# Hybrid diffusion backbone on one core: a written order for the opening, one-column norm sums, and unread products in two waits

## The chip, the core and the metric

The kernel runs on one core of a Trainium2 chip. A core has five engines that work side by side: TensorE (PE in the rows: matrix products, with PEld its loads of the stationary operand), VectorE (DVE), ScalarE (ACT), GpSimd (POOL) and SyncE (SP, which issues the DMAs). The metric is device time in microseconds (us) from one launch to its end, the median over runs. Lower is better.

## What is computed

Two layers of a diffusion backbone run over 256 latent tokens behind 256 context tokens, 1024 channels each, in float32. Cut to what matters here:

```python
def rms_norm(x, g):
    y = x * lax.rsqrt(jnp.mean(x * x, axis=-1, keepdims=True) + EPS)
    return y * g
def adaln(x, g, shift, scale):
    return rms_norm(x, g) * (1 + scale) + shift
...
    mod_x = jax.nn.silu(c) @ w_mod[l] + b_mod[l]        # nine vectors of 1024 per layer, for latent
    mod_c = jax.nn.silu(c_ctx) @ w_mod[l] + b_mod[l]    # and for context tokens
...
    x += 0.5 * gate1 * SwiGLU_1(adaln_1(x))             # norm 0 of the layer
    h  = adaln_2(x)                                     # norm 1
    x += gate2 * W_o(sum_b sigmoid(G_b h) * P_b(mixer_b(h)))
    x += 0.5 * gate3 * SwiGLU_2(adaln_3(x))             # norm 2
```

The last layer needs only the latent tokens behind its mixer. There are six norms in all, (layer, 0 to 2); each divides every token by the root of its mean square over the 1024 channels.

## The kernel before

Channels lie on the 128 partitions and tokens along the rows: the stream x is eight tiles (chunks c = 0 to 7) of 128 channels by 512 tokens, columns 0 to 255 context (segment s = 0) and 256 to 511 latent (segment 1). Every large product is made of three products of halves of float32 (`mm3`, lines 191 to 193), so each weight tile is first split by ScalarE (`wh`, line 150) and VectorE (`wl`, line 151). Nearly all the work is such products; weights are fetched in one written sequence (`plan`).

**Order.** The code emits instructions in one sequence. Small jobs (norm chains, attention) are put between products by a virtual clock: `later(ns, fn)` runs a job once the products emitted since then add up to ns (a 256-column term counts 320), `yield ns` does the same inside a job. After that the framework's scheduler may still move instructions by its own estimate of when they can start, and each engine runs its list in order.

**A norm.** While the last product of a block finishes chunk c of segment s, `residual` (line 399) adds it to x on VectorE, `norm_square` (line 302 on) squares it on ScalarE and adds it up on GpSimd (line 307) into `acc`; for chunks 6 and 7 the square goes to TensorE instead. `norm_sum` multiplies with a 128x32 block of ones (line 318), so that the sums over channels stand in a row, twice per segment: once with acc and chunk 6, once with chunk 7. `norm_chain` then scales (326), turns the row into a column with a transpose (329), copies it (331), raises it to the power -1/2 on GpSimd (333), and spreads it over 128 rows by a product with the identity (337). `norm_apply` makes h and its low half for eight chunks (351 to 353). The last two chunks are finished segment by segment (`finish_stream`): context 6, context 7, latent 6, latent 7; then the next block starts on the context half. Only norm (1, 2) has one segment and nothing to run beside its chain.

**The opening.** Norm (0, 0) needs the first four of 18 sets of modulation vectors, which TensorE makes from 8 MB of weights (`mod_set`: 64 small products a set, line 265; a copy, 268; a transpose, 270). `first_tiles` runs the first two tiles of the first feed-forward block chunk by chunk as each set comes: 96 products of 512 columns in all. The order in which the small and the large products stand on TensorE is the scheduler's.

Of the kernel before, what the change touches and what calls it, by code (L numbers as in the profile page):

```python
# [16 lines left out]
D = 1024  # L17
# [18 lines left out]
class Net:  # L36
# [151 lines left out]

    def mm3(self, ps, wh, wl, xh, xl, first, last):
        mm = self.nc.tensor.matmul  # L190
# [8 lines left out]
    def consts(self):  # L199
# [9 lines left out]
        self.sc = self.cp.tile([128, 8, 32], F32, name="sc")  # L209
        self.rows = self.cp.tile([128, 2, 2, 512], F32, name="rows")  # L210
# [48 lines left out]
    def mod_set(self, l, s):  # L259
        nc = self.nc  # L260
        ps = self.ps("D", (128, 128))
        for k in range(KC):
            w = self.first[s, k][:].rearrange("p (g n) -> p g n", g=4)
            for g in range(4):
                nc.tensor.matmul(ps[32 * g:32 * g + 32, :], self.sc[:, k, :], w[:, g, :], start=(k == 0),  # L265
                                 stop=(k == KC - 1), tile_position=(0, 32 * g))
        sb = self.half()[:, 0:128]
        nc.scalar.activation(sb, ps, AF.Copy)
        pt = self.ps("E", (128, 4, 32))
        nc.tensor.transpose(pt[:].rearrange("p g n -> p (g n)"), sb, self.ident)  # L270
# [8 lines left out]
    def norm(self, l, i, rng):  # L279
        segs = self.segs(rng)  # L280
        n = dict(l=l, i=i, segs=segs, ps={}, R={}, acc={})
        n["H"] = [tuple(self.hp.tile([128, NT], F32R, name=self.nm("h"), tag="h") for _ in range(2)) for _ in range(KC)]
        return n

    def norm_stat(self, n, c, s):
        nc = self.nc
        if c == 0:
            n["ps"][s] = self.ps("DE"[s], (64, 128))
        sq = self.half()
        nc.scalar.activation(sq, self.x[c][:, 256 * s:256 * s + 256], AF.Square)  # L290
        for t in range(2):
            nc.tensor.matmul(n["ps"][s][32 * t:32 * t + 32, :], self.ones, sq[:, 128 * t:128 * t + 128],
                             start=(c == 0), stop=(c == KC - 1), tile_position=(0, 32 * t))

    def norm_square(self, n, c, s):
# [15 lines left out]
    def norm_sum(self, n, s, c, sq):  # L311
        nc = self.nc
        if c == 6:
            n["ps"][s] = self.ps("DE"[s], (64, 128))
        for t in range(2):
            w = slice(128 * t, 128 * t + 128)
            for p, v in enumerate((n["acc"][s], sq) if c == 6 else (sq,)):
                nc.tensor.matmul(n["ps"][s][32 * t:32 * t + 32, :], self.ones, v[:, w], start=(c == 6 and p == 0),
                                 stop=(c == 7), tile_position=(0, 32 * t))
        if c == 7:  # L320
            self.job(self.norm_chain(n, s), (n["l"], n["i"], s))

    def norm_chain(self, n, s, R=None):
        nc = self.nc
        ms = self.small((64, 128), "ms", 2)
        nc.vector.tensor_scalar(ms, n["ps"][s], 1.0 / D, EPS, op0=ALU.mult, op1=ALU.add)
        yield 500
        pt = self.ps("C" if R is None else "A", (128, 2, 32))
        nc.tensor.transpose(pt[:].rearrange("p g n -> p (g n)"), ms, self.ident[:64, :64])
        v = self.small((128, 2), "v4")  # L330
        nc.vector.tensor_copy(v, pt[:, :, 0])
        r = self.small((128, 2), "r4")
        nc.gpsimd.tensor_tensor(r, v, self.mhalf.to_broadcast([128, 2]), op=ALU.pow)
        yield 2500 if s else 1900
        n["R"][s] = self.ps("DE"[s], (128, 256)) if R is None else R
        for t in range(2):
            nc.tensor.matmul(n["R"][s][:, 128 * t:128 * t + 128], r[:, t:t + 1].to_broadcast([128, 128]), self.ident,
                             start=True, stop=True)
        if R is None:
            for c in range(KC):  # L340
                self.norm_apply(n, c, s)
# [13 lines left out]
    def first_norm(self):  # L355
# [5 lines left out]
        for s in range(2):  # L361
            for _ in self.norm_chain(n, s, R[:, 256 * s:256 * s + 256]):
                pass

        def step(j):
            self.mod_set(0, j)
# [6 lines left out]
    def first_tiles(self, W, P, H):  # L373

        def terms(m, j):
            for k in (2 * j, 2 * j + 1):
# [659 lines left out]
```

## Time and profile before

| | |
|---|---|
| median of three runs | 2041.42 us (2040.87 to 2042.23) |
| the profiled execution, its own time | 2040.34 us |
| span in that profile | 2038.6 us |
| TensorE busy | 2010.8 us, 99% of the span |
| VectorE busy | 1331.3 us, 65% |
| ScalarE busy | 800.3 us, 39% |
| GpSimd busy | 87.3 us, 4% |
| DMA | 295.50 MB, mean 145 GB/s |
| mean granted TensorE clock | 0.997 of full speed |

Times inside the program are counted from the start of the span. A matmul's row shows its start and its modelled length; since matmuls overlap, what one costs is read from the distance between starts. Full speed of the granted clock is 2.4 GHz, and 0.50 is its other level, 1.2 GHz.

### The profile page before, as it was taken

To read this page: it belongs to the slowest core of one execution; us is meant where nothing else is said; L and a number is where in the kernel's file an instruction comes from. 1 tells how busy PE (TensorE), PEld (TensorE's weight loads), DVE (VectorE), ACT (ScalarE), POOL (GpSimd) and SP (SyncE) were. 2 spreads that over 40 slices of the span, in tenths; PEclk is the share of its full clock that TensorE was granted. 3 is DMA by queue.
4 is the path that set the end of the run, shared out by engine and by line. 5 is a ranking of instruction groups with operands and counts; after the bars stand their busy time and mean duration, and the time that the engine had idled before them with its cause. 6 is when DMAs were issued, how large, how long until landed. Compare 5 with 4: busy or idle time off the path is not lost.

```text
span 2038.6 us, 29838 instructions
## 1 busy us (share of the span) xinstructions
PE 2010.8 (99%) x11765; PEld 1732.7 (85%) x11765; DVE 1331.3 (65%) x2914; ACT 800.3 (39%) x1311; POOL 87.3 (4%) x90
## 2 busy tenths in 40 slices
PE   7999999999999999999999999999999999999999
PEld 4888887897797788888888888888888999999999
DVE  4878986667555545685733358689844788775554
ACT  3332232356444434232222333222323676664443
POOL 0000000120010000100000010000002101010000
PEclk9999999999999999999999999999999999999999
DMA  9554653522222224244532233446434324463453
GB/s 350 167 212 172 223 207 125 180 68 60 70 91 76 78 94 154 83 166 152 186 106 90 72 139 145 173 168 237 179 125 131 86 91 136 152 231 141 169 191 121
DMA packets 61549, 295.50 MB, mean 145 GB/s; under 512 B 14689, under 2 KB 16353, under 8 KB 38241
## 3 DMA queue, kind: packets, MB, share of 16 engines
q1 hardware_dynamic: 61408, 293.60, 41.4%
q8 instruction: 92, 1.51, 0.3%
q14 instruction: 49, 0.39, 0.1%
HBM read 292.53 MB, written 1.05 MB: 144 GB/s over the span
## 4 chain that ended last, share of the span: by engine, by line
PE 93%; DVE 3%; issue 2%; DMA 1%; ACT 1%; POOL 0%; SPq 0%; POOLq 0%; ACTq 0%; DVEq 0%
PE A L191 19%; PE A L192 18%; PE A L193 18%; PE B L191 11%; PE B L192 11%; PE B L193 11%; DVE a L249 1%; PE B L668 1%; PE D L682 1%; PE C L648 1%; PE E L719 1%; DVE wl L151 1%; DMA w<-in_dn 0%; ACT wh L150 0%; PE D L265 0%
## 5 line engine op out<-in xcount | busy, mean ns | idle before, releaser
L150 ACT ACTIVATE wh<-w 128x1024 fp32r<-128x1024 f32 (+2 forms) x476 | 428.1, 905 | 863.7 <-PE A L192 333.5
L151 DVE TENSOR_TENSOR wl<-w,wh 128x1024 fp32r<-128x1024 f32 (+2 forms) x476 | 490.1, 1033 | 286.5 <-ACT wh L150 283.6
L191 PE MATMUL A<-h,wh 128*128 128x512 f32 (+1 forms) x1440 | 506.9, 352 | 5.8 <-ACT wh L150 3.3
L193 PE MATMUL A<-h,wl 128*128 128x512 f32 (+1 forms) x1440 | 496.2, 345 | 1.2 <-DVE wl L151 1.1
L192 PE MATMUL A<-h,wh 128*128 128x512 f32 (+1 forms) x1440 | 496.3, 345 | 0.7 <-DVE h L353 0.7
L249 DVE CUSTOM_DVE_ANT_0 a<-w,rows 128x512 f32<-128x512 f32 x512 | 350.4, 695 | 41.1 <-DMA w<-in_mod 32.3
L191 PEld LDWEIGHTS A<-h,wh 128*128 128x128 f32 x1440 | 273.2, 190 | 48.3 <-issue 11.5
L193 PEld LDWEIGHTS A<-h,wl 128*128 128x128 f32 x1440 | 273.4, 190 | 35.1 <-DVE wl L151 2.5
L192 PEld LDWEIGHTS A<-h,wh 128*128 128x128 f32 x1440 | 273.5, 190 | 31.8 <-DVE h L353 1.4
L191 PE MATMUL B<-h,wh 128*128 128x512 f32 (+1 forms) x736 | 262.2, 356 | 0.0
L193 PE MATMUL B<-h,wl 128*128 128x512 f32 (+1 forms) x736 | 261.7, 356 | 0.0
L192 PE MATMUL B<-h,wh 128*128 128x512 f32 (+1 forms) x736 | 261.7, 356 | 0.0
L191 PEld LDWEIGHTS B<-h,wh 128*128 128x128 f32 x736 | 139.8, 190 | 19.9 <-ACT wh L150 0.4
L192 PEld LDWEIGHTS B<-h,wh 128*128 128x128 f32 x736 | 139.7, 190 | 19.6 <-issue 0.4
L193 PEld LDWEIGHTS B<-h,wl 128*128 128x128 f32 x736 | 139.6, 190 | 19.6
L432 DVE TENSOR_TENSOR t<-t,B 128x512 f32<-128x512 f32 (+1 forms) x88 | 54.2, 619 | 107.4 <-PE B L193 106.4
L307 POOL TENSOR_TENSOR nb<-nb,l 128x256 f32<-128x256 f32 x45 | 47.2, 1066 | 1320.0 <-ACT l L305 1320.0
L191 PE MATMUL A<-b,wh 128*128 128x512 f32 (+1 forms) x246 | 85.4, 347 | 1.0 <-ACT wh L150 1.0
L193 PE MATMUL A<-b,wl 128*128 128x512 f32 (+1 forms) x246 | 85.1, 346 | 1.1 <-DVE wl L151 1.1
L192 PE MATMUL A<-b,wh 128*128 128x512 f32 (+1 forms) x246 | 84.9, 345 | 0.0
L191 PE MATMUL B<-b,wh 128*128 128x512 f32 (+1 forms) x204 | 73.1, 358 | 0.4 <-ACT wh L150 0.4
L193 PE MATMUL B<-b,wl 128*128 128x512 f32 (+1 forms) x204 | 73.1, 358 | 0.3 <-DVE wl L151 0.3
(266 smaller groups left out, 2927.4 us busy)
## 6 DMA issues: line engine op xcount, KB each, us to landing
w<-in_gu SPq DMA_DIRECT2D x88, 1024.0 KB, 4.9
w<-in_mod SPq DMA_DIRECT2D x64, 1024.0 KB, 4.8
w<-in_dn SPq DMA_DIRECT2D x64, 704.0 KB, 4.1
w<-in_gb SPq DMA_DIRECT2D x64, 640.0 KB, 3.8
w<-in_fm SPq DMA_DIRECT2D x10, 1024.0 KB, 4.8
w<-in_tm SPq DMA_DIRECT2D x10, 1024.0 KB, 5.0
w<-in_wo SPq DMA_DIRECT2D x8, 1024.0 KB, 4.8
b<-in_first SPq DMA_DIRECT2D x20, 256.0 KB, 6.2
```

Of the source, the lines that this page charges most:

```text
L150: nc.scalar.activation(hi[i][:, :e], t[:, o:o + e], AF.Copy)
L151: nc.vector.tensor_tensor(lo[i][:, :e], t[:, o:o + e], hi[i][:, :e].bitcast(F32), op=ALU.subtract)
L191: mm(ps, wh, xh, start=first, stop=False)
L192: mm(ps, wh, xl, start=False, stop=False)
L193: mm(ps, wl, xh, start=False, stop=last)
L249: nc.vector.tensor_tensor_reduce(out=junk, in0=w[:, g, k], in1=self.rows[:, v, k], scale=1.0, scalar=0.0, op0=ALU.mult, op1=ALU.add, accum ...
L307: nc.gpsimd.tensor_tensor(n["acc"][s], n["acc"][s], sq, op=ALU.add)
L432: nc.vector.tensor_tensor(s[:, lo:hi], s[:, lo:hi], ps[1][:, lo:hi], op=ALU.mult)
L648: nc.tensor.transpose(pt[:, j], p[:, 128 * j:128 * j + 128], self.ident)
L668: nc.tensor.matmul(S[hh][:, 256 * j:256 * j + 256], queries(sg, j)[rows, pr, qw], keys(j, pr)[rows], start=True, stop=True)
L682: nc.tensor.matmul(y[64 * hh:64 * hh + 64, 128 * qb:128 * qb + 128], value(j, pr, hh), T[u, hh][:, j], start=(j == 0), stop=(j == n - 1), ...
L719: nc.tensor.matmul(pz[:, 256 * s:256 * s + 256], bd[:, 4 * j + k], U[c][:, src], start=True, stop=True)
```

## The change

It has four parts, and no weight, DMA or large product is added or left out.

1. **Opening.** `mod_set` is split into `mod_sums` (small products and copy) and `mod_set` (transpose and what follows), and `first_tiles` writes the order out by hand. While `pinned` is set, all its matmuls keep the written order. The spread of the first norm (`first_factors`) uses transposes.
2. **Norm sums.** In all later norms the 128 tokens become the stationary operand and one column of ones is multiplied, so that the sums come out as a column at once. The transpose and the copy of it go, and the spread (two products in two passes each) becomes two transposes of a broadcast column.
3. **GpSimd adds.** Norms behind feed-forward blocks (`pool`: norm 1 of both layers and norm 0 of layer 1) add all chunks on GpSimd and have one sum per segment; norm 2 adds chunks 0 to 6 there and gives the sum acc and chunk 7. The virtual waits become 2300 (or 1100) and 2600 or 4500.
4. **Unread products.** `warm(n, tag)` multiplies the identity by itself n times into a tile that nobody reads: 14 times while the first weights are split, and three times 5 in the chain of the one-segment norm (`alone`).

```diff
+    def pin(self, ins):
+        return self.tc.keep_in_program_order(ins)
...
-    def mod_set(self, l, s):
+    def mod_sums(self, s):
         nc = self.nc
         ps = self.ps("D", (128, 128))
         for k in range(KC):
             w = self.first[s, k][:].rearrange("p (g n) -> p g n", g=4)
             for g in range(4):
-                nc.tensor.matmul(ps[32 * g:32 * g + 32, :], self.sc[:, k, :], w[:, g, :], start=(k == 0),
-                                 stop=(k == KC - 1), tile_position=(0, 32 * g))
+                self.pin(nc.tensor.matmul(ps[32 * g:32 * g + 32, :], self.sc[:, k, :], w[:, g, :], start=(k == 0),
+                                          stop=(k == KC - 1), tile_position=(0, 32 * g)))
         sb = self.half()[:, 0:128]
         nc.scalar.activation(sb, ps, AF.Copy)
+        return sb
...
+    def token_sums(self, n, s, v, first, last):
+        if first:
+            n["ps"][s] = self.ps("DE"[s], (128, 2))
+        for t in range(2):
+            for i, q in enumerate(v):
+                self.nc.tensor.matmul(n["ps"][s][:, t:t + 1], q[:, 128 * t:128 * t + 128], self.ones[:, 0:1],
+                                      start=first and i + t == 0, stop=last and i + t == len(v))
+    def warm(self, n, tag):
+        t = self.ps(tag, (128, 128))
+        for _ in range(n):
+            self.pin(self.nc.tensor.matmul(t, self.ident, self.ident, start=True, stop=True))
...
+    def factors(self, n, s, v, R):
+        r = self.small((128, 2), "r4")
+        nc.gpsimd.tensor_tensor(r, v, self.mhalf.to_broadcast([128, 2]), op=ALU.pow)
+        n["R"][s] = R
+        return [lambda t=t: nc.tensor.transpose(R[:, 128 * t:128 * t + 128], r[:, t:t + 1].to_broadcast([128, 128]),
+                                                self.ident) for t in range(2)]
...
-        if c < 6:
+        if c < 7 or n["pool"]:
             nc.gpsimd.tensor_tensor(n["acc"][s], n["acc"][s], sq, op=ALU.add)
+        if c == 7:
+            v = [n["acc"][s]] if n["pool"] else [n["acc"][s], sq]
+            self.later(2300 if n["pool"] else 1100, lambda: self.norm_sum(n, s, v))
+    def norm_sum(self, n, s, v):
+        if n["alone"]:
+            self.warm(5, "D")
+        self.token_sums(n, s, v, True, True)
+        self.job(self.norm_chain(n, s), (n["l"], n["i"], s))
+    def norm_chain(self, n, s):
+        v = self.small((128, 2), "v4")
+        nc.vector.tensor_scalar(v, n["ps"][s], 1.0 / D, EPS, op0=ALU.mult, op1=ALU.add)
+        spread = self.factors(n, s, v, self.ps("DE"[s], (128, 256)))
+        if n["alone"]:
+            self.warm(5, "D")
         else:
-            self.later(1100, lambda: self.norm_sum(n, s, c, sq))
+            yield 4500 if s else 2600
+        for f in spread:
+            f()
+        if n["alone"]:
+            self.warm(5, "D")
...
-        self.first_step(0)
-        for j in range(4):
-            terms(0, j)
-            if j < 3:
-                self.first_step(j + 1)
-            terms(1, j)
+        self.pinned = True
+        self.first_step(0, self.mod_sums(0))
+        self.warm(14, "E")
+        terms(0, 0, 1)
+        terms(1, 0, 1)
+        self.first_step(1, self.mod_sums(1))
+        sb = self.mod_sums(2)
+        terms(0, 2)
+        self.first_step(2, sb)
+        terms(0, 3)
+        terms(1, 2, 3)
+        sb = self.mod_sums(3)
+        terms(0, 4)
+        self.first_step(3, sb)
+        terms(0, 5)
+        terms(1, 4, 5)
+        terms(0, 6, 7)
+        terms(1, 6, 7)
+        self.pinned = False
```

What this does to the lists of the engines is shown at three places. In the rows below, a name is a tile with its number, left of the arrow what is written and right of it what is read; the shape is the output.

First, TensorE in the opening, where the second set of modulation vectors (D_411 here) meets the first tile pair, before:

```order
L193 MATMUL B_341<-h_187,wl_317 128x512
L265 MATMUL D_411<-b_137,sc 32x128 x4
L265 MATMUL D_411<-b_139,sc 32x128 x4
L191 MATMUL A_342<-h_185,wh_322 128x512
L265 MATMUL D_411<-b_141,sc 32x128 x4
L192 MATMUL A_342<-h_186,wh_322 128x512
L193 MATMUL A_342<-h_185,wl_324 128x512
L191 MATMUL B_343<-h_185,wh_323 128x512
L265 MATMUL D_411<-b_143,sc 32x128 x4
L192 MATMUL B_343<-h_186,wh_323 128x512
```

The same set after the change (D_438), behind the last of the 24 products of chunks 0 and 1; the transpose of its copy is line 282:

```order
L196 MATMUL B_343<-h_187,wl_325 128x512
L273 MATMUL D_438<-b_137,sc 32x128 x4
L273 MATMUL D_438<-b_139,sc 32x128 x4
L273 MATMUL D_438<-b_141,sc 32x128 x4
L273 MATMUL D_438<-b_143,sc 32x128 x4
L273 MATMUL D_438<-ya_145,sc 32x128 x4
L273 MATMUL D_438<-ya_147,sc 32x128 x4
L273 MATMUL D_438<-ya_149,sc 32x128 x4
L273 MATMUL D_438<-ya_151,sc 32x128 x4
L282 MATMUL E_473<-cst,l_471 128x128
L273 MATMUL D_493<-yp_153,sc 32x128 x4
```

The small products stood between the large ones in pieces of four and now stand together; the transpose stands directly behind them.

Second, TensorE at norm (1, 0), context segment, while latent chunk 6 runs; before, the sum of chunk 7 and, six products on, the transpose (the sum of acc and chunk 6 stood further up):

```order
L193 MATMUL A_9832<-b_9018,wl_9752 128x256
L318 MATMUL D_9882<-l_9909,ones 32x128 x2
L191 MATMUL A_9832<-b_9085,wh_9750 128x256
L192 MATMUL A_9832<-b_9086,wh_9750 128x256
L193 MATMUL A_9832<-b_9085,wl_9752 128x256
L191 MATMUL A_9832<-b_9152,wh_9750 128x256
L192 MATMUL A_9832<-b_9153,wh_9750 128x256
L193 MATMUL A_9832<-b_9152,wl_9752 128x256
L329 MATMUL C_9933<-cst,ms_9925 128x64
```

After, the one sum of that segment, 24 products behind chunk 7's last (12 before):

```order
L196 MATMUL A_9825<-m_9279,wh_9744 128x256
L196 MATMUL A_9825<-m_9280,wh_9744 128x256
L196 MATMUL A_9825<-m_9279,wl_9746 128x256
L303 MATMUL D_9925<-ones,nb_9530 128x1 x2
L196 MATMUL A_9825<-m_9346,wh_9744 128x256
```

One sum of acc alone (nb) stands where two sums and a transpose stood before.

Third, TensorE at the one-segment norm (1, 2), before, from the last product of chunk 7 to the first of the next block:

```order
L193 MATMUL B_16316<-a_16082,yp_16230 128x256
L318 MATMUL E_16356<-l_16374,ones 32x128 x2
L329 MATMUL C_16384<-cst,ms_16382 128x64
L337 MATMUL E_16390<-cst,r_16388 128x128 x2
L191 MATMUL A_16378<-h_12878,wh_16239 128x256
```

The same place after the change:

```order
L196 MATMUL B_16285<-a_16051,yp_16199 128x256
L310 MATMUL D_16345<-cst 128x128 x5
L303 MATMUL E_16351<-ones,nb_16091 128x1
L303 MATMUL E_16351<-ones,l_16339 128x1
L303 MATMUL E_16351<-ones,nb_16091 128x1
L303 MATMUL E_16351<-ones,l_16339 128x1
L310 MATMUL D_16361<-cst 128x128 x5
L339 MATMUL E_16358<-cst,r_16359 128x128 x2
L310 MATMUL D_16369<-cst 128x128 x5
L196 MATMUL A_16343<-h_12850,wh_16208 128x256
```

Unread products now stand in each of the three waits of that chain, and the transpose (329) is gone.

## Rows read from the trace of the kernel before

**Rows 1.** First part of the page: busy time, share, instructions.

```profile
PE 2010.8 (99%) x11765; PEld 1732.7 (85%) x11765; DVE 1331.3 (65%) x2914; ACT 800.3 (39%) x1311; POOL 87.3 (4%) x90
```

**Rows 2.** Windows: length, busy us of each engine, granted clock, DMA.

```profile
20.50:27.30 6.80, 5.80 (x20) 3.91 (x24) 6.01 (x8) 4.30 (x6) 0.00 (x0) 0.50 1.02 371
60.77:350.00 289.23, 289.23 (x1277) 239.56 (x1276) 235.96 (x572) 80.21 (x103) 0.00 (x0) 1.00 0.53 189
1843.20:1846.60 3.40, 3.04 (x14) 3.04 (x15) 3.40 (x10) 2.58 (x6) 0.00 (x0) 0.50 0.00 0
```

**Rows 3.** Timeline of TensorE, opening: start, length, instruction, idle before.

```profile
21.50 0.80 PE L191 MATMUL A<-h,wh 128*128 128x512 f32 x1 [3.34 <-ACT wh L150]
...
27.72 0.49 PE L191 MATMUL A<-h,wh 128*128 128x512 f32 x1
28.14 0.43 PE L265 MATMUL D<-b,sc 128*32 128x128 f32 x8
28.50 0.50 PE L192 MATMUL A<-h,wh 128*128 128x512 f32 x1
...
34.35 0.33 PE L270 MATMUL E<-cst,l 128*128 128x128 f32 x1 [0.46 <-ACT l L268]
...
48.78 1.51 PE L265 MATMUL D<-b,sc 128*32 128x128 f32 x46
...
60.77 0.40 PE L191 MATMUL A<-h,wh 128*128 128x512 f32 x1
```

**Rows 4.** Timeline of VectorE, opening: the last weight splits of the first pair.

```profile
24.15 2.36 DVE L151 TENSOR_TENSOR wl<-w,wh 128x1024 fp32r<-128x1024 f32 x2
```

**Rows 5.** Timeline of TensorE at two norms: products around each interruption.

```profile
426.32 0.28 PE L193 MATMUL A<-h,wl 128*128 128x256 f32 x1
...
426.78 0.28 PE L192 MATMUL A<-h,wh 128*128 128x256 f32 x1
...
1203.07 0.28 PE L193 MATMUL A<-b,wl 128*128 128x256 f32 x1
...
1203.85 0.28 PE L192 MATMUL A<-b,wh 128*128 128x256 f32 x1
...
1206.87 0.28 PE L193 MATMUL B<-b,yp 128*128 128x256 f32 x1
...
1207.55 0.28 PE L192 MATMUL B<-b,ya 128*128 128x256 f32 x1
...
1208.38 0.28 PE L193 MATMUL B<-b,yp 128*128 128x256 f32 x1
...
1209.38 0.28 PE L192 MATMUL B<-b,ya 128*128 128x256 f32 x1
...
1217.82 0.28 PE L192 MATMUL B<-h,wh 128*128 128x256 f32 x1
...
1218.46 0.28 PE L191 MATMUL A<-h,wh 128*128 128x256 f32 x1
...
1218.70 0.28 PE L193 MATMUL A<-h,wl 128*128 128x256 f32 x1
1219.33 0.71 PE L337 MATMUL E<-cst,r 128*128 128x128 f32 x4 [0.35 <-POOL r L333]
```

**Rows 6.** Timeline of TensorE, norm (0, 2), context segment.

```profile
834.07 0.30 PE L318 MATMUL D<-l,ones 128*32 128x128 f32 x1 [1.71 <-ACT l L305]
```

**Rows 7.** Timeline of TensorE at the one-segment norm (1, 2).

```profile
1838.20 0.28 PE L193 MATMUL B<-a,yp 128*128 128x256 f32 x1
1839.56 0.41 PE L318 MATMUL E<-l,ones 128*32 128x128 f32 x4 [1.08 <-ACT l L305]
...
1841.67 0.71 PE L337 MATMUL E<-cst,r 128*128 128x128 f32 x4 [1.04 <-POOL r L333]
1843.56 0.58 PE L191 MATMUL A<-h,wh 128*128 128x256 f32 x1 [1.18 <-ACT h L352]
```

**Rows 8.** Instructions of two lines: count, ns least/median/most, first and last start.

```profile
L307 POOL TENSOR_TENSOR nb<-nb,l x45: 729/1074/1472, 354.7 to 1833.5; 128x256 f32<-128x256 f32 x45
L249 DVE CUSTOM_DVE_ANT_0 a<-w,rows x512: 671/691/1232, 62.6 to 1488.0; 128x512 f32<-128x512 f32 x171
```

More of the change, by code (lines that the diff above doesn't have):

```diff
@@ L209, in consts @@
         self.sc = self.cp.tile([128, 8, 32], F32, name="sc")
+        self.sv = self.sc[:, :, 0:2]
         self.rows = self.cp.tile([128, 2, 2, 512], F32, name="rows")
@@ L264, in mod_set @@
             for g in range(4):
-                nc.tensor.matmul(ps[32 * g:32 * g + 32, :], self.sc[:, k, :], w[:, g, :], start=(k == 0),
-                                 stop=(k == KC - 1), tile_position=(0, 32 * g))
+                self.pin(nc.tensor.matmul(ps[32 * g:32 * g + 32, :], self.sc[:, k, :], w[:, g, :], start=(k == 0),
+                                          stop=(k == KC - 1), tile_position=(0, 32 * g)))
         sb = self.half()[:, 0:128]
         nc.scalar.activation(sb, ps, AF.Copy)
+        return sb
+    def mod_set(self, l, s, sb):
+        nc = self.nc
         pt = self.ps("E", (128, 4, 32))
-        nc.tensor.transpose(pt[:].rearrange("p g n -> p (g n)"), sb, self.ident)
+        self.pin(nc.tensor.transpose(pt[:].rearrange("p g n -> p (g n)"), sb, self.ident))
         bm = self.par[l][:, O_BM + 4 * s:O_BM + 4 * s + 4]
@@ L280, in norm @@
         segs = self.segs(rng)
-        n = dict(l=l, i=i, segs=segs, ps={}, R={}, acc={})
+        n = dict(l=l, i=i, segs=segs, ps={}, R={}, acc={}, pool=i != 2, alone=len(segs) == 1)
         n["H"] = [tuple(self.hp.tile([128, NT], F32R, name=self.nm("h"), tag="h") for _ in range(2)) for _ in range(KC)]
         return n
+    def token_sums(self, n, s, v, first, last):
[9 more added lines that the diff above has]
+            self.pin(self.nc.tensor.matmul(t, self.ident, self.ident, start=True, stop=True))
     def norm_stat(self, n, c, s):
@@ L293, in norm_stat, with first_factors @@
                              start=(c == 0), stop=(c == KC - 1), tile_position=(0, 32 * t))
+    def first_factors(self, n, s, R):
+        nc = self.nc
+        ms = self.small((64, 128), "ms", 2)
+        nc.vector.tensor_scalar(ms, n["ps"][s], 1.0 / D, EPS, op0=ALU.mult, op1=ALU.add)
+        pt = self.ps("A", (128, 2, 32))
+        nc.tensor.transpose(pt[:].rearrange("p g n -> p (g n)"), ms, self.ident[:64, :64])
+        v = self.small((128, 2), "v4")
+        nc.vector.tensor_copy(v, pt[:, :, 0])
+        for f in self.factors(n, s, v, R):
+            f()
+    def factors(self, n, s, v, R):
+        nc = self.nc
+        r = self.small((128, 2), "r4")
[3 more added lines that the diff above has]
+                                                self.ident) for t in range(2)]
     def norm_square(self, n, c, s):
@@ L305, in norm_square @@
         nc.scalar.activation(sq, x, AF.Square)
-        if c < 6:
+        if c < 7 or n["pool"]:
             nc.gpsimd.tensor_tensor(n["acc"][s], n["acc"][s], sq, op=ALU.add)
-        else:
-            self.later(1100, lambda: self.norm_sum(n, s, c, sq))
[L311 to L341, printed above, removed]
+        if c == 7:
+            v = [n["acc"][s]] if n["pool"] else [n["acc"][s], sq]
+            self.later(2300 if n["pool"] else 1100, lambda: self.norm_sum(n, s, v))
@@ new lines, in norm_sum @@
+    def norm_sum(self, n, s, v):
[4 more added lines that the diff above has]
+    def norm_chain(self, n, s):
+        nc = self.nc
+        v = self.small((128, 2), "v4")
+        nc.vector.tensor_scalar(v, n["ps"][s], 1.0 / D, EPS, op0=ALU.mult, op1=ALU.add)
+        spread = self.factors(n, s, v, self.ps("DE"[s], (128, 256)))
+        if n["alone"]:
+            self.warm(5, "D")
+        else:
+            yield 4500 if s else 2600
+        for f in spread:
+            f()
+        if n["alone"]:
+            self.warm(5, "D")
+        for c in range(KC):
+            self.norm_apply(n, c, s)
+        if n["alone"]:
+            yield 0
@@ L361, in first_norm, with step @@
         for s in range(2):
[L362 to L366, printed above, removed]
+            self.first_factors(n, s, R[:, 256 * s:256 * s + 256])
+        def step(j, sb):
+            self.mod_set(0, j, sb)
             for c in (2 * j, 2 * j + 1):
@@ L373, in first_tiles, with terms @@
     def first_tiles(self, W, P, H):
-        def terms(m, j):
-            for k in (2 * j, 2 * j + 1):
+        def terms(m, *ks):
+            for k in ks:
                 for g in range(2):
                     self.term(P[m][g], W[m], 1024 * g, H, *ALL, k)
-        self.first_step(0)
-        for j in range(4):
-            terms(0, j)
-            if j < 3:
-                self.first_step(j + 1)
-            terms(1, j)
+        self.pinned = True
[17 more added lines that the diff above has]
+        self.pinned = False
     def finish_stream(self, parts, last, add, nxt):
```

3 lines of the change are left out of this document (2 added, 1 removed).

## The prediction

> **What bounds it now.** I read the engine table first. TensorE is busy 99% of the span and VectorE 65% [rows 1], so only two things can move the time: what TensorE executes beside the large products, and the places where it runs slowly or waits. The windows show both. From 60.77 to 350.00 us TensorE has not one idle moment: 289.23 us busy over 1277 products of 512 columns, 0.2265 us each, at a granted clock of 1.00, while VectorE is busy 82% [rows 2]. Two short stretches differ: 20.50 to 27.30 us, with 5.80 us of work at clock 0.50, and 1843.20 to 1846.60 us, with 3.04 us, also at 0.50 [rows 2]. The first lies behind a wait of 3.34 us, the second behind three waits of 1.08, 1.04 and 1.18 us [rows 3, 7]. The timeline of TensorE then gives the cost of every interruption as the distance between the products around it. The change touches three such places, the opening, six norms and one of these six that stands alone. I cost each and add them up.
>
> **The opening.** From the first large product (21.50) to the first of the third tile (60.77) it lasts 39.27 us [rows 3]. In it stand 96 products of 512 columns, 96 × 0.2265 = 21.7 us, and the sums of three sets, 192 passes. A run of 46 takes 1.51 us, one pass alone about 0.27 by its shape, so 0.0276 us for each further one [rows 3], 5.3 us together. The other 12.2 us are loss, of three kinds. The clock: the 5.80 us of work at half speed would take 2.9, loss 2.9 us. Switching: from 27.72 to 28.50 stand one large product and 8 small ones, 0.78 us where 0.23 + 0.22 would do: 0.33 us for each interruption. There are 14 such groups up to 48.78, two of them shown [rows 3]; loss 4.6 us. The rest, 4.7 us, is waiting, for copies (0.46 at 34.35) and for h.
>
> After the change the small products of a set stand together: three interruptions, 1.0 us. The 28 unread passes (14 products of two) at the 0.11 us of an fp32 pass of 128 columns (0.45 / 4, below) take 3.1 us and so fit inside the 3.34 us wait. If they keep the clock up the 2.9 us come back. But the first products are then too early for their weights: the splits of the first pair end at 26.51, and the third and fourth of them run 1.18 us each from 24.15 [rows 4]. Laying 24 products at 0.2265 against these ends gives about 28.1 instead of 26.9 us for the last, 1.2 us lost. The three copies and transposes now stand ahead of products in a fixed order, so I keep the waits as they are, 4.4 us with that 1.2 in it. The loss falls from 12.2 to 5.4, and the third tile starts at 54.0: **gain 6.8 us**. Bounds: nothing, if the fixed order waits as often as the free one switched, and 12 if all loss goes. Since TensorE never idles from 60.77 to 350 [rows 2], an earlier start arrives later in full, as long as VectorE, with its 82%, keeps up.
>
> **The norm sums.** Two neighbouring products are 0.23 us of normal distance over two steps (2 × 0.2265 / 2). What exceeds it is the price, all from [rows 5]. The sum of acc and chunk 6 costs 1.00 − 0.23 = 0.77, the sum of chunk 7 0.78 − 0.23 = 0.55, the transpose of the row 0.64 − 0.23 = 0.41, the spread with its four passes 0.68 − 0.23 = 0.45, thus 0.11 for a pass. Ahead of the latent spread comes a wait, 0.63 − 0.11 = 0.52, of which its row puts 0.35 on GpSimd's power.
>
> A segment costs 2.18 us, the latent one 2.70. Four norms have two segments: 4 × 4.88 = 19.5, and norm (0, 2) waited 1.71 us more for the square of a chunk [rows 6]: 21.2 us before.
>
> After, a spread is two transposes of 128 columns; a pair of those costs 0.46 − 0.23 = 0.23 [rows 5]. No row shows a one-column product with 128 stationary rows. It lies between the 0.0276 us of a small pass [rows 3] and 0.22, if load and product lie one behind the other at 0.11 each. I take 0.11, the price of a 128-column pass, because loading 128 stationary columns is then the longer part. The three GpSimd norms have per segment two products of two passes, 0.45, and the spread 0.23: 6 × 0.68 = 4.1. The remaining norm has four products, 0.90 + 0.23, twice: 2.3. Together 6.4 us, a saving of 14.8.
>
> New waits come off. In the written order the sum at a GpSimd norm stands 24 products behind chunk 7's last, 24 × 0.113 = 2.7 us. In that time residual, square and a GpSimd add of 0.73 to 1.47 us, median 1.07 [rows 8], must pass. The add leaves the other two 1.2 us or more, which may just do, and I leave 0.1 us for each of six. In norm (0, 2) the first sum stands 12 products back and the second spread 8 behind its sum, 0.9 us against a scale, a power and their turns: 0.5 each. That makes 1.6 us. **Gain 13.2 us.** Bounds of the pass price on 48 passes: 4 us more (0.0276), 5.3 less (0.22).
>
> **The lone norm (1, 2).** From its last product to the next block 5.36 us pass (1838.20 to 1843.56), in three waits of 1.08, 1.04 and 1.18 [rows 7]. Five unread products are 10 passes, 1.1 us at full clock: they fit each wait. If the clock stays up, the 3.40 us window at 0.50 shrinks to half: 1.7 us. The chain loses the transpose and its copy (0.41 plus a turn), and 0.22 of spread, and gets two more sum passes: about 0.6 shorter. The early sum of acc and chunk 6 (0.77) goes. **Gain 3.1 us.** Bounds: 1.4, if the clock still falls, to 4.
>
> **Sum.** 6.8 + 13.2 + 3.1 = 23.1 us. The profiled execution took 2040.34, 1.74 above its span, and lies 1.08 below the median of the runs. So 2040.34 − 23.1 = 2017.2, and as a median 2018.3 us. VectorE loses 12 instructions, SyncE's list keeps its order, ScalarE's nearly; GpSimd goes from 4% of the span to some 5%, with 15 adds of 1.1 us more [rows 1, 8]. None of these is a price by itself.
>
> **Rivals.** The clock is not held (0.10): unread products or the order leave the granted clock at 0.50 in 21 to 27 us and at 1843. Against it: TensorE fell to 0.50 behind a wait of 3.34 us and behind waits of about 1.1 in a row [rows 2, 3, 7], and these are filled. For it: the fill is inferred at 0.11 a pass, and if shorter, a wait is left. Loss: 2.9 + 1.7, and the 58 unread passes at half clock take 0.11 more each, 6.4 us, of which half may stick out of the waits: 2023 to 2026.
>
> GpSimd and VectorE hinder each other (0.12). GpSimd's adds range from 0.73 to 1.47 us and VectorE's modulation rows, usually 0.69, reach 1.23 [rows 8]. If 15 more adds each cost VectorE 0.54 and all of it came onto TensorE, that is 8.1 us: 2026.4. Against it: in most norms VectorE has slack. The Trainium skill ("SBUF — State Buffer", section "SBUF: two separate sides") says that the port pair which VectorE and GpSimd share is an exclusive lock, taken against each other by a GpSimd operation and a VectorE operation with two SBUF inputs, and that the loser fully blocks. The spread of those two rows agrees with such a lock, but no row shows it, and the residuals that lead into the sums are of that kind.
>
> The opening's gain is swallowed (0.10): modulation products, paced by transfers or by VectorE at 82%, stall TensorE further on. Against it: no idle from 60.77 to 350 [rows 2]. Price 6.8: 2025.1.
>
> Slower than before (0.02). TensorE's list has its order, and when it comes to a sum the latent residual of chunk 7 still queues on VectorE behind the 13 or so operations (by the order) that normalise the context half; square and GpSimd add follow, and TensorE stands. It decides from a wait of about 4.5 us at each of six sums: (23.1 + 4) / 6. Against it: 51 products, 5.8 us, lie between the end of chunk 7 and the latent sum. With 5 us each: 2018.3 + 30 = 2048.
>
> The written order brings nothing in the opening and the lone norm (0.05): 2018.3 − 13.2 kept, the rest lost: 2028.
>
> **Chances and range.** My forecast has 0.61. About 0.2% or 4 us is what a measurement of this kernel can tell from no change. All cases but the slower one, and small mixtures of two misses, lie more than 4 us below 2041.42: faster 0.95, same 0.03, slower 0.02. The range of the forecast alone is 2014 to 2024 (pass price, −4 to +5.3). With the opening's upper bound at the low end and the rivals at 2023 to 2028 in it, and about one tenth left out at each end, it is 2013 to 2029.
>
> **What would show it.** Granted clock 1.00 through 17 to 28 us and at 1843; third tile at about 54; no transpose of the row, sum groups at 0.45 and 0.90; waits for GpSimd ahead of spreads gone, except about 0.5 at norm (0, 2); at norm (1, 2) about 4.7 us from last to first product; TensorE without idle from 54 to 345. I am wrong if sums or unread passes cost over 0.2 us each, if an idle stretch appears at the new sums, or if the third tile starts after 58.

## The result, and the profile after

The changed kernel takes **2020.64 us** (median of four runs, 2020.27 to 2021.12), against 2041.26 us for the kernel before in the same session: a ratio of 0.9898 with a 95% interval from 0.9886 to 0.9910, 20.6 us less. The forecast was 2018.3, with a range from 2013 to 2029. The span of the profiled execution falls from 2038.6 to 2019.2 us.

Both traces hold the same 10,518 large products on TensorE. Numbering them in order of time and subtracting the start of the k-th one after from that of the k-th one before gives the lead of the changed kernel, and the places at which it grows:

| place | lead grows by | forecast |
|---|---|---|
| opening (5.03 us at the third tile's first product, 5.47 from 58 us on) | 5.47 us | 6.8 us |
| norm (0, 1) | 2.69 | |
| norm (0, 2) | 3.79 | |
| norm (1, 0) | 2.30 | |
| norm (1, 1) | 2.73 | |
| these four norms together | 11.51 | 13.2 |
| attention of the second layer | −0.24 | 0 |
| norm (1, 2), one segment | 2.46 | 3.1 |
| all | 19.2 | 23.1 |

Between these places the lead stays constant to 0.05 us, but for swings between 355 and 375 us that cancel. The rows of the changed kernel follow. First the page's engine table and three windows (length, then busy us of PE, PEld, DVE, ACT, POOL, the granted clock, DMA share and GB/s), which answer to [rows 1, 2]:

```profile
PE 1997.5 (99%) x11732; PEld 1732.6 (86%) x11732; DVE 1329.5 (66%) x2905; ACT 799.8 (40%) x1311; POOL 102.5 (5%) x105
```

```profile
20.50:27.30 6.80, 6.09 (x32) 4.63 (x31) 6.10 (x8) 4.46 (x6) 0.00 (x0) 1.00 1.01 363
...
60.00:300.00 240.00, 240.00 (x1061) 198.72 (x1060) 205.12 (x503) 65.63 (x83) 0.00 (x0) 1.00 0.57 202
...
1825.55:1828.60 3.05, 3.05 (x25) 2.94 (x25) 3.05 (x9) 2.23 (x5) 0.00 (x0) 1.00 0.00 0
```

Both stretches that ran at a granted clock of 0.50 now show 1.00, and from 60 to 300 us TensorE still never idles, so what the opening wins is kept. TensorE is busy 13.3 us less. Its timeline in the opening, to be held against [rows 3]:

```profile
18.46 3.39 PE L310 MATMUL E<-cst 128*128 128x128 f32 x28 [0.26 <-DVE mods L284]
21.66 0.72 PE L196 MATMUL A<-h,wh 128*128 128x512 f32 x2
...
28.62 1.08 PE L273 MATMUL D<-b,sc 128*32 128x128 f32 x32
...
34.43 0.42 PE L273 MATMUL D<-a,sc 128*32 128x128 f32 x8 [0.90 <-DMA a<-in_first]
...
50.68 0.50 PE L196 MATMUL A<-h,wh 128*128 128x512 f32 x1 [0.71 <-DVE h L393]
...
54.67 0.61 PE L196 MATMUL A<-h,wh 128*128 128x512 f32 x2
```

The 28 unread passes fill the wait of 3.34 us, 0.11 us each, and the third tile starts at 54.67 (forecast 54.0). New is the wait for a transfer: at 34.43 TensorE stands 0.90 us for the last weights of the third set. For the stretch from the first large product to the third tile's first one, the windows of the kernel before and of the changed kernel are (length, then TensorE's busy time first):

```profile
21.50:59.70 38.20, 35.90 (x291) 23.30 (x292) 20.10 (x66) 12.92 (x22) 1.01 (x1) 0.92 0.79 294
```

```profile
21.66:54.67 33.01, 30.04 (x293) 22.86 (x293) 21.81 (x67) 14.14 (x24) 1.01 (x1) 1.00 0.90 337
```

TensorE is busy 5.86 us less there and idle 0.67 us more (2.97 for 2.30).

Next TensorE at the latent segment of norm (0, 1), at the context sum and the latent spread of the mixer's norm (0, 2), and at the first h of norm (1, 0); these answer to [rows 5, 6]:

```profile
403.71 0.28 PE L196 MATMUL B<-wh,h 128*128 128x256 f32 x1
403.83 0.51 PE L303 MATMUL E<-ones,nb 128*128 128x1 f32 x4
404.20 0.36 PE L196 MATMUL B<-wh,h 128*128 128x256 f32 x1
404.40 0.28 PE L196 MATMUL B<-wl,h 128*128 128x256 f32 x1
...
406.44 0.28 PE L196 MATMUL A<-h,wl 128*128 128x256 f32 x1
406.56 0.38 PE L339 MATMUL E<-cst,r 128*128 128x128 f32 x2
406.69 0.48 PE L196 MATMUL A<-h,wh 128*128 128x256 f32 x2
407.01 0.28 PE L196 MATMUL A<-h,wl 128*128 128x256 f32 x1
...
416.51 0.51 PE L196 MATMUL B<-wh,h 128*128 128x256 f32 x2 [0.47 <-DVE h L393]
...
826.83 0.28 PE L196 MATMUL A<-b,yp 128*128 128x256 f32 x1
...
828.07 0.28 PE L196 MATMUL A<-b,yp 128*128 128x256 f32 x1
...
841.29 0.43 PE L339 MATMUL E<-cst,r 128*128 128x128 f32 x2 [0.35 <-POOL r L337]
...
1198.31 0.39 PE L196 MATMUL A<-h,wh 128*128 128x256 f32 x1 [0.26 <-ACT h L392]
```

A sum with two one-column products costs 404.40 − 403.71 − 0.23 = 0.46 us, a spread 407.01 − 406.44 less three products of 0.12, 0.21; the sum of the mixer's norm (eight passes between 826.83 and 828.07, three products off) 0.88. No wait stands ahead of the latent spread any more except in norm (0, 2). But 10 us behind the spread of norm (0, 1), at 416.51, TensorE waits for a low half of h.

Last the one-segment norm (1, 2), against [rows 7]: from the last product of chunk 7 to the first of the next block TensorE has no idle moment, and 4.85 us pass instead of 5.36.

```profile
1820.70 0.28 PE L196 MATMUL B<-a,yp 128*128 128x256 f32 x1
1820.82 1.27 PE L310 MATMUL D<-cst 128*128 128x128 f32 x10
1821.93 0.28 PE L303 MATMUL E<-ones,nb 128*128 128x1 f32 x2
...
1823.95 0.41 PE L339 MATMUL E<-cst,r 128*128 128x128 f32 x2
...
1825.55 0.39 PE L196 MATMUL A<-h,wh 128*128 128x256 f32 x1
```

### The profile page after: what moved, and what is told of

Same layout as the page of the kernel before. It is cut to its first block, busy times and chain, and to the rows that moved or that the text cites. A ratio compares the mean times of both kernels' runs of the same rounds, so it can differ in the third digit from the quotient of the medians.

```text
span 2019.2 us, 29778 instructions
## 1 busy us (share of the span) xinstructions
PE 1997.5 (99%) x11732; PEld 1732.6 (86%) x11732; DVE 1329.5 (66%) x2905; ACT 799.8 (40%) x1311; POOL 102.5 (5%) x105
## 4 chain that ended last, share of the span: by engine, by line
PE 93%; DVE 3%; DMA 2%; issue 1%; ACT 1%; POOL 0%; SPq 0%; ACTq 0%; POOLq 0%; DVEq 0%
PE A L196 56%; PE B L196 32%; DVE a L256 1%; DMA b<-in_first 1%; PE B L721 1%; PE D L735 1%; PE C L701 1%; DVE wl L151 1%; PE E L772 1%; DMA w<-in_dn 0%; DMA par<-in_par 0%; PE E L638 0%; DMA yp<-in_first 0%; ACT wh L150 0%; DVE x L452 0%
## 5 line engine op out<-in xcount | busy, mean ns | idle before, releaser
L196 PE MATMUL A<-h,wh 128*128 128x512 f32 (+1 forms) x2880 | 750.3, 348 | 1.3 <-DVE h L393 0.7
L196 PEld LDWEIGHTS A<-h,wh 128*128 128x128 f32 x2880 | 496.6, 189 | 73.5 <-issue 10.9
L196 PE MATMUL B<-h,wh 128*128 128x512 f32 (+1 forms) x1472 | 397.5, 355 | 0.0
L196 PE MATMUL A<-b,wh 128*128 128x512 f32 (+1 forms) x492 | 126.3, 346 | 1.8 <-ACT wh L150 1.8
L196 PE MATMUL B<-b,wh 128*128 128x512 f32 (+1 forms) x408 | 110.7, 358 | 0.0
L196 PEld LDWEIGHTS A<-b,wh 128*128 128x128 f32 x492 | 85.9, 189 | 13.9 <-ACT wh L150 2.7
L196 PE MATMUL A<-wh,h 128*128 128x256 f32 x448 | 84.9, 287 | 0.0
L196 PEld LDWEIGHTS B<-b,wh 128*128 128x128 f32 x408 | 72.8, 189 | 11.2
L196 PE MATMUL A<-m,wh 128*128 128x512 f32 (+1 forms) x280 | 72.8, 347 | 0.0
L196 PEld LDWEIGHTS A<-wh,h 128*128 128x128 f32 x448 | 71.0, 191 | 0.2
```

The source lines that it names most:

```text
L196: mm = lambda *a, **k: self.pin(self.nc.tensor.matmul(*a, **k)) if self.pinned else self.nc.tensor.matmul(*a, **k)
```

## The experiments

Each kernel was timed beside the kernel before, and the gain against that is given, since the medians of before differ by 0.7 us between sessions. The changed kernel's own gain is 20.6 us. Differences under about 1 us are read from the traces, by the lead described above. A trace shows one execution, and the opening differs between executions: in the seven traces with the changed kernel's opening the third tile starts anywhere from 53.8 to 54.9 us.

### The opening: order or clock

**no_fill_open** leaves out the unread products of the opening.

```diff
-        self.warm(14, "E")
```

> The changed kernel without the 14 unread products of the opening. Theory (they hold the clock): the granted clock falls to 0.50 from about 21.6 us as before the change; some 13 products run at 0.43 instead of 0.23 us, but the first of them wait for their weights anyway, so 24 products end near 29.7 instead of 28.5 us and the time rises by about 1.2 us, to 2021.8. Rival (the written order alone is the gain, the clock is of no account there): clock 0.50 may show, but the third tile starts where it did and the time stays at 2020.6.

Measured: 2021.38 us, 20.1 us less than before. Its window and the timeline of TensorE behind the first 24 large products:

```profile
20.50:27.30 6.80, 5.77 (x15) 4.12 (x16) 5.85 (x8) 4.28 (x5) 0.00 (x0) 0.59 1.02 361
```

```profile
29.52 1.08 PE L273 MATMUL D<-b,sc 128*32 128x128 f32 x32
...
33.09 1.06 PE L273 MATMUL D<-a,sc 128*32 128x128 f32 x32
34.17 1.13 PE L196 MATMUL A<-h,wh 128*128 128x512 f32 x2
```

The clock falls, to 0.59 in the mean, and the second set's sums start 0.90 us later (29.52 against 28.62). But the sums of the third set then find their weights there and don't wait, and by 36.3 us both kernels stand at the same product. The third tile starts no later (lead 0.29 us the other way, less than executions differ). My theory falls: the unread products of the opening hold the clock and win nothing that these runs can tell.

**double_fill_open** takes 28 in place of 14.

```diff
-        self.warm(14, "E")
+        self.warm(28, "E")
```

> The changed kernel with 28 instead of 14 unread products in the opening. Theory (an unread fp32 pass of 128 columns costs 0.11 us and stands on the path as soon as the wait is filled): 28 passes more, 3.1 us, of which 1.2 us may hide in the wait for the first weights' low halves: 2022.5 to 2023.7. Rival (the opening has slack behind it, in the transfer of the last sets): no change, 2020.6.

Measured: 2023.28 us (2021.99 to 2024.72), 18.2 less, which the theory covers, but not where it said. In the trace the first large product starts 2.79 us later than in the changed kernel, the 31st 0.66, and the third tile 0.3. The trace shows 1.2 us more far behind the opening, nearly all at two places: 0.72 us at 175 us, where a weight's transfer lands late (ScalarE can split it from 173.60, in the changed kernel from 170.85) and TensorE waits for its low half, and 0.36 at 1802, behind VectorE. That the unread products bring these about is not shown. So some 2.5 us of slack lie ahead of the third tile, most of it ahead of the third set's products, as the run without unread products says too.

**free_order** keeps the unread products and gives the order back to the scheduler.

```diff
-        self.pinned = True
         self.first_step(0, self.mod_sums(0))
         self.warm(14, "E")
-        terms(0, 0, 1)
...
+        for j in range(4):
+            terms(0, 2 * j, 2 * j + 1)
+            if j < 3:
+                self.first_step(j + 1, self.mod_sums(j + 1))
+            terms(1, 2 * j, 2 * j + 1)
```

> The changed kernel with the opening in the order of before, left to the scheduler, but with the 14 unread products. Theory (grouping saves the switching between large and small products): small products stand in some 14 pieces again, the third tile starts about 3 us later at full clock, time 2023.7. Rival (the whole gain of the opening is the clock): third tile where it was, 2020.6.

Measured: 2026.77 us, 14.7 less than before. The trace loses 5.3 us by the 91st product and 5.8 by the 121st. In this execution the unread passes ran partly at half clock (granted 0.66 in the mean) and stuck out of the wait:

```profile
18.30 5.02 PE L310 MATMUL E<-cst 128*128 128x128 f32 x28 [0.26 <-DVE mods L284]
```

The first large product came 1.4 us late, which the slack above may or may not have swallowed in this order; 4.4 to 5.8 us are the order's.

**order_only** is the kernel before with the new order of the opening alone (no unread products, old norms), and **norms_only** the changed kernel with the opening of before.

```diff
+        self.pinned = True
+        self.first_step(0, self.mod_sums(0))
+        terms(0, 0, 1)
+        terms(1, 0, 1)
+        self.first_step(1, self.mod_sums(1))
+        sb = self.mod_sums(2)
...
+        self.pinned = False
```

> The kernel before with the written order of the opening alone, without unread products and with the norms of before. Theory, as it stands after the run without the 14 unread products (the order alone is the gain of the opening, the clock's part is taken back by the wait for the third set): granted clock 0.50 to 0.60 from 20.5 to 27.3 us, and still 5.5 us won: 2035.9. Rival (order and clock each carry half): 3 us won, 2038.4.

> The changed kernel with the opening in the order of before and without its 14 unread products: the norm sums, GpSimd's adds and the one-segment norm alone. Theory (the parts add up): 19.2 less 5.5 us won, 13.7, and 2027.6. Rival (a part of the opening's gain is given back later, so that the norms alone are worth more): 2025 or less.

Measured: order_only 2035.50 us, ratio 0.9973 (0.9962 to 0.9983), 5.7 us less; norms_only 2027.44, ratio 0.9929 (0.9917 to 0.9941), 13.7 us less. In order_only the clock is low in the first window; the second runs from the first large product to the third tile:

```profile
20.50:27.30 6.80, 5.50 (x16) 3.90 (x17) 6.27 (x9) 4.45 (x6) 0.00 (x0) 0.63 1.03 380
...
21.76:54.25 32.49, 31.46 (x292) 24.03 (x292) 21.90 (x68) 14.04 (x24) 1.01 (x1) 0.94 0.90 343
```

The lead at the end is still 5.5 us. So the order alone is worth the whole gain of the opening, and the parts add up within the noise: 5.7 + 13.7 = 19.4 us. The second window says where the order's gain lies: against the kernel before TensorE is busy 4.4 us less and idle 1.3 us less (31.46 and 1.03 for 35.90 and 2.30). The unread products take another 1.4 us off the busy time (30.04), and the idle time grows by 1.9 (2.97).

### The one-segment norm

**lone_no_fill** leaves out its three runs of unread products.

```diff
-        if n["alone"]:
-            self.warm(5, "D")
```

> The changed kernel without the three runs of unread products in norm (1, 2). Theory (they hold the clock): granted clock 0.50 for the first products of the next block, 14 of them 0.09 us dearer, 1.3 us lost, and 0.2 us won since the chain no longer waits for unread products: 2021.7. Rival (the shorter chain is the gain and the unread products only lengthen it): 2020.4.

Measured: 2021.87 us (2020.41 to 2023.56), 19.6 less, so 1.0 us worse than the changed kernel by the medians. The profiled execution was the slowest of the four; in it 2.1 us are lost in this norm, twice the forecast. The window, and the first product of the next block:

```profile
1825.00:1830.00 5.00, 3.87 (x18) 3.87 (x19) 4.94 (x13) 3.33 (x7) 0.00 (x0) 0.50 0.01 3
```

```profile
1826.13 0.58 PE L196 MATMUL A<-h,wh 128*128 128x256 f32 x1 [1.18 <-ACT h L386]
```

That product starts 5.11 us behind the last one of chunk 7 (4.85 with unread products), and the granted clock stays at 0.50 up to 1830, for some 20 products 0.21 us apart instead of 0.12. So here, where the next block follows with nothing to wait for, the unread products are worth 2.1 us by this trace and 1.0 by the medians. Without them the early sum and the shorter chain still win 0.76 and 0.25 us, of which 0.66 go again, since the low clock lasts some 20 products here and 14 in the kernel before.

### The norm sums, and the waits behind them

**no_gpsimd_last** never adds chunk 7's square on GpSimd, **gpsimd_02** does so in norm (0, 2) too.

```diff
-        n = dict(l=l, i=i, segs=segs, ps={}, R={}, acc={}, pool=i != 2, alone=len(segs) == 1)
+        n = dict(l=l, i=i, segs=segs, ps={}, R={}, acc={}, pool=False, alone=len(segs) == 1)
...
+        n = dict(l=l, i=i, segs=segs, ps={}, R={}, acc={}, pool=len(segs) == 2, alone=len(segs) == 1)
```

> The changed kernel with the last square of each segment never added on GpSimd (all norms take acc and chunk 7 as norm 2 does, with its place of the sum). Theory (a pass costs 0.11 us on TensorE, GpSimd's add is hidden): six sums cost 0.89 instead of 0.45 us, 2.6 us lost, less the 0.5 us that two sums waited in norm (1, 0): 2022.7. Rival (GpSimd's adds hold up VectorE and the sums): VectorE's operations beside them get shorter, the waits for h go, and the time is 2020 or less.

> The changed kernel with all chunks added on GpSimd in norm (0, 2) too (the one-segment norm stays as it is). Theory: two sums cost 0.45 instead of 0.89 us, and the longer chain meets the later place of the sum: 0.9 us won, 2019.7; if the latent spread still waits 0.5 us, no more is won. Rival (the chain through square, GpSimd add, scale and power is then too long for the mixer's end): TensorE stands before the sum or before the first h, a loss of 0.5 to 2 us: 2021 to 2022.5.

Measured: no_gpsimd_last 2020.57 us, 21.3 less than before; gpsimd_02 2023.85, 18.0 less. In no_gpsimd_last, for which the theory said 2022.7, six sums do cost 0.44 us more, 2.6 us in all, but at the end the trace stands only 0.45 us behind: the waits for h in norms (0, 1), (1, 0) and (1, 1) are gone, since the spreads stand sooner by the products around them (1.4 us in the latent segment of norm (0, 1)). So adding the last chunk on GpSimd, with the later place that it asks of the sum, is worth about half a microsecond by the trace and nothing that the timing can tell; this run does not part the two. In gpsimd_02, slower than theory and rival both allowed, the latent sum stands in TensorE's list before its data are there:

```profile
833.77 0.60 PE L303 MATMUL E<-ones,nb 128*128 128x1 f32 x4 [2.50 <-POOL nb L354]
```

```profile
831.86 0.48 DVE L452 SCALAR_TENSOR_TENSOR x<-B,G,x 128x256 f32<-128x256 f32 x1
```

```profile
832.99 0.72 POOL L354 TENSOR_TENSOR nb<-nb,l 128x256 f32<-128x256 f32 x1 [3.17 <-ACT l L352]
```

Residual at 831.86, add from 832.99, sum at 833.77: 2.50 us idle. Behind this wait the clock falls as well, and some 15 products of the next block stand 0.21 us apart instead of 0.12, 1.3 us more:

```profile
834.90:838.00 3.10, 3.10 (x17) 3.10 (x16) 3.10 (x10) 2.03 (x4) 0.00 (x0) 0.50 0.00 0
```

This is the rival with which the kernel would have become slower, at one place and, in the wait alone, at a little over half of the price it needed.

**spread_sooner** and **spread_as_before** write the spreads sooner behind the sums.

```diff
-            yield 4500 if s else 2600
+            yield 3900 if s else 2600
...
+            yield 3000 if s else 2400
```

> The changed kernel with the latent spread written 600 units of the virtual clock sooner (3900 instead of 4500). Theory (the wait of 0.6 us that the changed kernel shows in norms (0, 1) and (1, 1), 10 us behind the spread, comes from VectorE's list: the last low half of h stands behind a normalisation of attention that waits for GpSimd, and behind a weight split): that low half now stands ahead of both, the two waits go and the time falls by 1.2 us, to 2019.4. Rival (the wait only moves): the spread now waits for GpSimd's power, 0.3 to 0.5 us in each norm, and the time stays within 0.5 us of 2020.6.

> The changed kernel with the spreads as soon behind the sums as in the kernel before (3000 and 2400 units). Theory (the later places are worth what the waits of before cost): a wait of about 0.5 us for GpSimd's power stands ahead of each latent spread again, the waits for h go; against the kernel with 4500 units four times 0.5 lost and 1.2 to 1.7 won: 2020.6 to 2021.5. Rival (the chain without transpose and copy is short enough for the old places): no wait at either, 2019.

Measured: 2019.90 us, 21.9 less, and 2020.20, 21.6 less. First VectorE in the changed kernel behind the latent spread of norm (0, 1), then the same in spread_sooner:

```profile
414.50 0.43 DVE L644 TENSOR_TENSOR m<-m,rs 128x256 f32<-128x256 f32 x1 [1.12 <-POOL rs L631]
414.84 1.22 DVE L151 TENSOR_TENSOR wl<-w,wh 128x1024 fp32r<-128x1024 f32 x1
415.98 0.48 DVE L393 SCALAR_TENSOR_TENSOR h<-l,mods,h 128x256 fp32r<-128x256 f32 x1
```

```profile
413.12 0.48 DVE L393 SCALAR_TENSOR_TENSOR h<-l,mods,h 128x256 fp32r<-128x256 f32 x1
...
414.50 0.42 DVE L644 TENSOR_TENSOR m<-m,rs 128x256 f32<-128x256 f32 x1 [0.82 <-POOL rs L631]
...
415.82 2.55 DVE L151 TENSOR_TENSOR wl<-w,wh 128x1024 fp32r<-128x1024 f32 x2
```

In the changed kernel the last low half of h (L393) stands behind an operation that waited 1.12 us for GpSimd and behind a weight split of 1.22, and TensorE waits for it until 416.51. In spread_sooner it stands ahead of both and the wait is gone, in norm (0, 1) and in (1, 1): 0.73 and 0.72 us of lead, as the theory says. In spread_as_before waits for GpSimd's power come back ahead of three latent spreads, 0.4 us twice and 0.9 in norm (1, 0), whose row is

```profile
1204.72 0.43 PE L339 MATMUL E<-cst,r 128*128 128x128 f32 x2 [0.72 <-POOL r L337]
```

and its context spread, sooner too, takes away the wait at 1198.31. So both theories are seen at once: a spread that is too soon waits, one that is too late loses its place on VectorE.

**tuned** puts together what these runs point to.

```diff
-            yield 4500 if s else 2600
+            yield 3900 if s else 2400
...
-            self.warm(5, "D")
+            self.warm(4, "D")
```

> The changed kernel with the latent spread at 3900 and the context spread at 2400 units, and runs of 4 instead of 5 unread products in norm (1, 2). Theory: the two waits of 0.6 us in norms (0, 1) and (1, 1) go as in the run with 3900 alone; in norm (1, 0) the context normalisation stands ahead of a modulation row on VectorE and the 0.42 us for the first h go; in norm (1, 2) 6 passes fewer stand on TensorE, 0.3 to 0.6 us, at a clock that stays 1.00: together 2 us, 2018.5. Rival (the waits move, or the clock falls with shorter runs): 2019.9 or more, with clock 0.50 behind norm (1, 2).

Measured: **2018.22 us** (2018.06 to 2018.68), 23.0 less than before, ratio 0.9886 (0.9873 to 0.9900). Its interval overlaps that of the changed kernel; the trace says where 2.8 us of lead come from: 0.7 in each of the norms (0, 1) and (1, 1), 0.8 in (1, 0), the rest in the opening, where nothing was changed, so that 0.65 us of its gain are chance. Norm (1, 2) wins nothing: TensorE now waits there for h, at a clock that stays 1.00.

```profile
1822.72 0.39 PE L196 MATMUL A<-h,wh 128*128 128x256 f32 x1 [0.29 <-ACT h L392]
```

## Why the prediction held, and where its steps were off

**The opening: 5.5 us for 6.8, and in part for another reason.** Three things were off. The mark at 60.77 us was not the third tile's first product: it is the 100th large product, 99 stand ahead of it and not 96, so 0.7 us of the "loss" was work. The waits "as they are" were 4.7 us, and with 1.2 more they are 5.9, not 4.4; summed so, the forecast would have been 5.3 us, close to the 5.5 measured, but by luck, for 2.9 of them are the clock's. That step, "if they keep the clock up the 2.9 us come back", failed: the clock was kept, and the time was not. What the full clock wins in the first 24 products is waited for again, most of it at the third set's weights (0.90 us at 34.43) and at h (0.71 at 50.68); order_only has the whole gain at clock 0.63. The step on switching carried the forecast: 14 interruptions by 0.33 us became three, 3.6 us. Of the 4.4 us of busy time that order_only saves, its shorter stretch at clock 0.50 makes about 1 (an estimate from the granted clocks of 0.50 and 0.63), which leaves 3.4. The other part, 1.3 us less idle, was not forecast; that it comes from the sums of a set standing together, so that its h starts sooner, is argued and not shown. That the gain is not swallowed later was right: the lead of 5.47 us stays to the microsecond's hundredth from 65 to 340 us.

**The norm sums: 11.5 for 13.2.** The prices were right: 0.46, 0.88 and 0.21 us measured for 0.45, 0.90 and 0.23 forecast, and a one-column pass costs the 0.11 us of a 128-column one. (The Trainium skill, "TensorE: Matmul & The Clock Gate", section "LDWEIGHTS (loading the stationary operand)", says that a load takes the number of stationary columns divided by 1.2, in ns; an estimate of 107 ns from it agrees with the row.) What failed is the term "new waits, 1.6 us": I looked for them at the six GpSimd sums and at the sum and the spread of norm (0, 2). There they cost 1.0 us: 0.4 at the two sums of norm (1, 0) and 0.6 at the latent spread of norm (0, 2), while its sums wait for nothing. More stands where I did not look, at the products that read h: 0.63 us in each of the norms (0, 1) and (1, 1) and 0.42 in (1, 0) beyond the normal distance. The later place of the spread, costed at nothing, moved the normalisation behind other work in VectorE's list; spread_sooner and tuned show it by taking the waits away. Another 0.37 us is lost in norm (0, 2), where TensorE is to write into tile A again and VectorE's residual still reads it. TensorE's load of the stationary operand for that product, and the residual:

```profile
825.42 0.19 PEld L196 LDWEIGHTS A<-b,ya 128*128 128x128 f32 x1 [0.32 <-DVE x L452]
```

```profile
824.89 0.47 DVE L452 SCALAR_TENSOR_TENSOR x<-A,G,x 128x256 f32<-128x256 f32 x1
```

The residual stands behind two modulation rows that took 1.23 and 1.10 us beside GpSimd adds (median 0.69). A row was slow there in the kernel before too, but TensorE then stood at the sum [rows 6]; with that wait gone, this one shows.

**The one-segment norm: 2.46 for 3.1.** The early sum gave 0.76 us as forecast and the chain 0.5 for 0.6. The clock was over-sized: at clock 0.50 a 256-column product takes 0.21 us and at full clock 0.12, so the 14 or so slow products cost 1.2 us and not half of the window, 1.7. That the unread products hold the clock there is shown by lone_no_fill.

**The rivals.** In the runs without unread products the clock was lost, and its price was 0 in the opening and 2.1 us in norm (1, 2), less than the 4.6 to 7.8 that the rival named. That GpSimd and VectorE hinder each other was true at single places (below) and cost 0.37 us in norm (0, 2), and part of the wait in norm (1, 0). The residuals, which the prediction counted among the hindered operations, are not: they read one tile from PSUM. The waiting sum of the "slower" rival did not occur in the changed kernel, whose sums stand 24 products back, and occurred with 2.5 us in gpsimd_02, where the mixer's end leaves less room. The case "the order brings nothing" is refuted by order_only.

**Still open.** Double_fill_open is 1.9 us slower than no_fill_open by the medians and 1.4 by the spans. The trace shows where the difference grows behind the opening (a late transfer at 175 us, a wait at 1802), but not whether the unread products are behind it. Runs of one kernel here differ by 1 to 4 us, so it may be no more than that.

## What to carry to other kernels

Work that is cut from the busiest engine pays in full only if every later member of its chain keeps its place: after moving a step, look at what now stands ahead of its successors on the engines that are not full. A filled wait pays where full-speed work follows at once and nothing else comes late; where the next wait is a transfer, a fast start is only a longer wait. Small and large products on TensorE should stand in groups: here 0.33 us were lost at each interruption of the large ones.

## What the hardware showed unasked

**An exclusive turn between GpSimd and VectorE, in rows.** Rows 8 had only hinted at it. In norm (1, 0) of the changed kernel, VectorE and then GpSimd:

```profile
1194.95 1.22 DVE L151 TENSOR_TENSOR wl<-w,wh 128x1024 fp32r<-128x1024 f32 x1
1196.09 1.23 DVE L256 CUSTOM_DVE_ANT_0 a<-w,rows 128x512 f32<-128x512 f32 x1
```

```profile
1195.63 1.14 POOL L354 TENSOR_TENSOR nb<-nb,l 128x256 f32<-128x256 f32 x1 [1.56 <-ACT l L352]
```

The add starts at 1195.63 beside a weight split that ends at 1196.17, and takes 1.14 us where the least is 0.73: 0.41 more, so 0.60 of its undisturbed 0.73 us lie behind the split. The modulation row begins at 1196.09, beside the add that lasts to 1196.77, and takes 1.23 where the median is 0.69: 0.54 more, so 0.55 of its 0.69 us lie behind the add. All three read two operands from SBUF. The Trainium skill ("SBUF — State Buffer", section "SBUF: two separate sides") says that such operations take an exclusive lock and the loser blocks; these rows agree, and the modulation row so delayed stood just ahead of the context normalisation for whose h TensorE waited at 1198.31. A residual on VectorE reads one tile from PSUM instead, and is not held up; here one runs inside an add:

```profile
1809.50 0.48 DVE L452 SCALAR_TENSOR_TENSOR x<-B,G,x 128x256 f32<-128x256 f32 x1
```

```profile
1808.83 1.14 POOL L354 TENSOR_TENSOR nb<-nb,l 128x256 f32<-128x256 f32 x1 [2.67 <-ACT l L352]
```

Three residuals of the changed kernel meet an add so, and take 0.47 to 0.48 us, their usual length.

**The clock does not always stay full during the unread products.** In free_order the same 28 passes took 5.02 us at a mean granted clock of 0.66, and not 3.39 at 1.00, and stuck out of the wait by 1.4 us, so the length of such a filling is not fixed by its count. In the other seven traces with 28 passes there they took 3.39 us each time. The clock was 1.00 from 14 to 18.3 us, ahead of the passes, in free_order too; why it fell stays open.
